# Windowed attention: 256 rows per transfer, manual order, values one block late, and stores moved to another queue

## The chip, the cores and the metric

The kernel runs on one core of a Trainium2 chip; the other cores are idle. Its engines go by the profile's names: PE does the matrix products, ACT and DVE the element-wise work, POOL and SP issue transfers, and 16 DMA engines move the data. A transfer is cut into packets that are spread over these 16; here nearly every data packet is one row of a tile, or two neighbouring rows in e4 and e6. A queue is named by the engine that issues to it. The metric is the device time of one execution in microseconds (us), median of several runs. All runs quoted here of one kernel agree within 0.3%.

## The reference

Attention inside windows of 64 rows, over float32 inputs of shape 4 x 4096 x 1536:

```python
q_w, k_w, v_w = (x.reshape(B, S // 64, 64, D) for x in (q, k, v))      # B, S, D = 4, 4096, 1536
logits = np.einsum('bnwd,bnud->bnwu', q_w, k_w) * D ** -0.5
attn = softmax(logits, axis=-1)
out = np.einsum('bnwu,bnud->bnwd', attn, v_w)
```

Three inputs are read and one output is written, each 100.66 MB: 402.65 MB at the HBM (off-chip memory) in all.

## The kernel before

It handles 128 blocks of 128 rows (two windows). Each block is loaded by three transfers that the POOL engine issues and that convert float32 to float16 on the way. q and k are transposed on PE, their score product is taken for both windows at once, exp is taken of the two 64 x 64 diagonal squares, and the value product is done per window. The store goes out some blocks later, on the POOL queue too.

```python
def load(blk):
    ...                                             # q16, k16, v16: FP16 tiles, 3 buffers
    nc.gpsimd.dma_start(out=q16, in_=qb[blk]...)    # casts float32 -> float16
    nc.gpsimd.dma_start(out=k16, in_=kb[blk]...)
    nc.gpsimd.dma_start(out=v16, in_=vb[blk])

for blk in range(NBLK):                             # NBLK = 128
    ...                                             # load(blk), NPRE = 2 ahead at the start
    if len(pending_store) > 2:
        bs, ts = pending_store.pop(0)
        nc.gpsimd.dma_start(out=ob[bs], in_=ts)     # float32, plain copy
    ...                                             # transposes, scores, exp
    for j in range(D // 512):
        o = o_ps.tile([128, 512], FP32, tag="o", name="o")
        nc.tensor.matmul(o[0:64, :], lhsT=et[0:64, 0:64], rhs=v16[0:64, sl], tile_position=(0, 0), ...)
        nc.tensor.matmul(o[64:128, :], lhsT=et[64:128, 64:128], rhs=v16[64:128, sl], tile_position=(64, 64), ...)
        ...                                         # scaled by 1/sum into out_sb, ACT and DVE in turn
    pending_store.append((blk, out_sb))
for bs, ts in pending_store:                        # the last three
    nc.sync.dma_start(out=ob[bs], in_=ts)
```

The softmax here doesn't subtract the row's maximum and nothing guards it: scores larger than these inputs give would overflow.

## Time and profile before

| | before |
|---|---|
| time, median of 3 runs (the comparison below has a fourth) | 967.0 us |
| span of the profiled run | 964.4 us |
| PE / ACT / DVE busy | 76% / 39% / 31% |
| longest chain | 94% DMA |

From the page of the kernel before: the DMA row over 40 slices of the span (9 is 90% or more busy), the packet counts, the queues (q0 is POOL's, q1 SP's; packets, MB written, share of 16 engines), the HBM traffic and the chain that ended last.

```profile
DMA  9999999999999999999999999999999999999997
DMA packets 73795, 252.60 MB, mean 262 GB/s; under 512 B 8192, under 2 KB 8192, under 8 KB 73728
q0 software_dynamic: 73296, 249.33, 104.6%
q1 hardware_dynamic: 432, 2.36, 0.6%
HBM read 301.99 MB, written 100.66 MB: 417 GB/s over the span
DMA 94%; issue 4%; PE 1%; POOL 0%; DVE 0%; ACT 0%; POOLq 0%; ACTq 0%; DVEq 0%
```

The 16 DMA engines are busy until the last of the 40 slices, so what counts is what they deliver. The 8,192 packets under 512 bytes are completions (16 for each of 512 transfers). The timeline of POOL in the middle of the run (start, duration, engine and line, idle before and what ended it) gives the pace:

```profile
450.27 0.53 POOL L55 DMA_DIRECT2D q<-in_q_dram  x1 [1.22 <-PE o L139]
452.10 0.53 POOL L56 DMA_DIRECT2D k<-in_k_dram  x1 [1.30 <-DMA k<-in_k_dram]
453.96 0.53 POOL L57 DMA_DIRECT2D v<-in_v_dram  x1 [1.33 <-DMA v<-in_v_dram]
455.94 0.54 POOL L86 DMA_DIRECT2D out_dram<-out_sb  x1 [1.45 <-DMA out_dram<-out_sb]
457.86 0.53 POOL L55 DMA_DIRECT2D q<-in_q_dram  x1 [1.38 <-DMA q<-in_q_dram]
```

Four transfers, 786,432 bytes each at the HBM side, take about 7.4 us on average. The end of the run, as busy time by stretch (the last three numbers are PE's granted clock, the DMA share and GB/s written):

```profile
954.00:956.00 2.00, 1.90 (x19) 1.74 (x18) 0.69 (x1) 0.54 (x1) 0.00 (x0) 0.50 0.62 246
956.00:958.00 2.00, 1.56 (x17) 1.22 (x15) 0.69 (x1) 0.71 (x2) 0.00 (x0) 0.79 0.45 183
958.00:960.00 2.00, 1.20 (x8) 0.41 (x8) 0.92 (x2) 1.38 (x4) 0.00 (x0) 1.00 0.05 15
960.00:962.00 2.00, 0.00 (x0) 0.00 (x0) 0.00 (x0) 0.27 (x1) 0.00 (x0) 0.56 0.48 197
```

Here the loads are over, the last block is computed, and the DMA engines run dry until its store.

### The profile page before, as it was taken

What the parts mean: (1) busy time and instruction counts of PE and PEld (TensorE: products, weight loads), DVE (VectorE), ACT (ScalarE), POOL (GpSimd) and SP (SyncE); (2) the same over time, 40 slices, a digit from 0 to 9 for tenths busy, and PEclk for the clock granted to TensorE, in tenths of its full rate; (3) what the DMA queues carried; (4) which work ended last, traced back from release to release, by engine and by line L of the source; (5) the groups of instructions that cost most, each with busy time, mean ns of one, the idle gap of its engine ahead of it and who ended that gap; (6) DMA issues with size and microseconds to landing.
All of it is one profiled execution on the core that took longest, in us unless ns stands there. A gap on an engine that the chain in (4) does not pass through costs nothing.

```text
span 964.4 us, 14246 instructions
## 1 busy us (share of the span) xinstructions
PE 731.4 (76%) x5632; PEld 510.0 (53%) x5632; DVE 294.6 (31%) x515; ACT 378.1 (39%) x641; POOL 271.1 (28%) x514
## 2 busy tenths in 40 slices
PE   5667778787687877877878777777787777878775
PEld 3445555555455555555555555544555555555553
DVE  2323332333333333323233333323332323323332
ACT  3434343433333443434343433344343333344333
POOL 4222222222222222222222322322222222222220
PEclk9776575756756666566575755766656556565655
DMA  9999999999999999999999999999999999999997
GB/s 182 253 270 269 261 261 268 270 262 261 266 270 264 261 266 268 266 262 265 266 267 262 266 264 267 264 266 264 265 267 266 264 264 267 266 264 263 267 268 224
DMA packets 73795, 252.60 MB, mean 262 GB/s; under 512 B 8192, under 2 KB 8192, under 8 KB 73728
## 3 DMA queue, kind: packets, MB, share of 16 engines
q0 software_dynamic: 73296, 249.33, 104.6%
q1 hardware_dynamic: 432, 2.36, 0.6%
q8 instruction: 44, 0.72, 0.3%
q14 instruction: 23, 0.19, 0.0%
HBM read 301.99 MB, written 100.66 MB: 417 GB/s over the span
## 4 chain that ended last, share of the span: by engine, by line
DMA 94%; issue 4%; PE 1%; POOL 0%; DVE 0%; ACT 0%; POOLq 0%; ACTq 0%; DVEq 0%
DMA k<-in_k_dram 92%; DMA q<-in_q_dram 1%; PE tp L95 1%; DVE xt L97 0%; POOL q L55 0%; PE o L135 0%; PE lt L103 0%; PE o L139 0%; POOLq L56 0%; POOL v L57 0%; DVE out_sb L146 0%; ACT out_sb L144 0%; ACT et L112 0%; ACTq L177 0%; PE sp L120 0%
## 5 line engine op out<-in xcount | busy, mean ns | idle before, releaser
L95 PE MATMUL tp<-ident,k 128*128 128x128 f16 x1536 | 327.7, 305 | 139.6 <-DMA k<-in_k_dram 139.6
L95 PE MATMUL tp<-ident,q 128*128 128x128 f16 x1536 | 341.1, 296 | 28.8 <-DMA q<-in_q_dram 12.1
L95 PEld LDWEIGHTS <-k 128*128 128x128 f16 x1536 | 205.9, 139 | 205.3 <-DMA k<-in_k_dram 167.9
L97 DVE COPY xt<-tp 128x1024 f16<-128x1024 f16 x256 | 177.0, 691 | 392.4 <-PE tp L95 392.2
L95 PEld LDWEIGHTS <-q 128*128 128x128 f16 x1536 | 199.8, 137 | 89.8 <-DMA q<-in_q_dram 50.9
L99 ACT COPY xt<-tp 128x1024 f16<-128x1024 f16 x128 | 129.5, 1012 | 287.2 <-PE tp L95 287.2
L144 ACT ACTIVATE out_sb<-o,rs 128x512 f32<-128x512 f32 x256 | 168.6, 685 | 98.7 <-PE o L139 95.1
L103 PE MATMUL lt<-xt 128*128 128x128 f16 x1536 | 192.9, 295 | 3.0 <-DVE xt L97 1.8
L103 PEld LDWEIGHTS <-xt 128*128 128x128 f16 x1536 | 150.6, 136 | 27.4 <-DVE xt L97 26.5
L135 PE MATMUL o<-v,et 64*64 64x512 f16 x384 | 150.6, 502 | 0.0
L139 PE MATMUL o<-v,et 64*64 64x512 f16 x384 | 144.6, 498 | 0.0
L57 POOL DMA_DIRECT2D v<-in_v_dram x128 | 67.9, 530 | 178.1 <-DMA v<-in_v_dram 135.0
L86 POOL DMA_DIRECT2D out_dram<-out_sb x125 | 67.2, 537 | 173.5 <-DMA out_dram<-out_sb 134.0
L112 ACT ACTIVATE et<-lt,zeros 64x64 f16<-64x64 f32 x128 | 39.6, 309 | 192.4 <-PE lt L103 192.4
L56 POOL DMA_DIRECT2D k<-in_k_dram x128 | 67.9, 530 | 162.6 <-DMA k<-in_k_dram 162.6
L55 POOL DMA_DIRECT2D q<-in_q_dram x128 | 68.0, 531 | 156.2 <-PE o L139 124.0
L146 DVE TENSOR_SCALAR out_sb<-o,rs 128x512 f32<-128x512 f32 x128 | 96.0, 750 | 46.6 <-PE o L139 45.1
L129 DVE RECIPROCAL rs<-sp 128x1 f32<-128x1 f32 x128 | 21.5, 168 | 225.5 <-PE sp L124 221.0
L120 PE MATMUL sp<-ones,et 64*64 64x1 f16 x128 | 25.3, 198 | 56.5 <-ACT et L112 56.5
L120 PEld LDWEIGHTS <-et 64*64 64x64 f16 x128 | 14.4, 113 | 86.7 <-ACT et L112 86.2
L139 PEld LDWEIGHTS <-et 64*64 64x64 f16 x384 | 39.4, 132 | 16.8 <-issue 9.8
L135 PEld LDWEIGHTS <-et 64*64 64x64 f16 x384 | 43.5, 126 | 0.4
(12 smaller groups left out, 81.5 us busy)
## 6 DMA issues: line engine op xcount, KB each, us to landing
out_dram<-out_sb POOLq DMA_DIRECT2D x125, 768.0 KB, 14.2
q<-in_q_dram POOLq DMA_DIRECT2D x128, 384.0 KB, 14.3
k<-in_k_dram POOLq DMA_DIRECT2D x128, 384.0 KB, 14.3
v<-in_v_dram POOLq DMA_DIRECT2D x128, 384.0 KB, 14.3
out_dram<-out_sb SPq DMA_DIRECT2D x3, 768.0 KB, 7.8
```

The costliest lines, as they stand in the source:

```text
L55: nc.gpsimd.dma_start(out=q16, in_=qb[blk].rearrange("p (c e) -> p c e", e=128))
L56: nc.gpsimd.dma_start(out=k16, in_=kb[blk].rearrange("p (c e) -> p c e", e=128))
L57: nc.gpsimd.dma_start(out=v16, in_=vb[blk])
L86: nc.gpsimd.dma_start(out=ob[bs], in_=ts)
L95: nc.tensor.transpose(tp[:, i, :], src, ident)
L97: nc.vector.tensor_copy(out=xt[:, g * 8 : g * 8 + 8, :], in_=tp)
L99: nc.scalar.copy(out=xt[:, g * 8 : g * 8 + 8, :], in_=tp)
L103: nc.tensor.matmul(lt[:, 0:128], lhsT=xt[:, 2 * c + 1, :], rhs=xt[:, 2 * c, :], start=(c == 0), stop=(c == DC - 1),)
L135: nc.tensor.matmul(o[0:64, :], lhsT=et[0:64, 0:64], rhs=v16[0:64, sl], tile_position=(0, 0), start=True, stop=True,)
L139: nc.tensor.matmul(o[64:128, :], lhsT=et[64:128, 64:128], rhs=v16[64:128, sl], tile_position=(64, 64), start=True, stop=True,)
L144: nc.scalar.activation(out_sb[:, sl], o, copy_f, bias=0.0, scale=rs)
L146: nc.vector.tensor_scalar_mul(out_sb[:, sl], o, scalar1=rs)
```

## The change

The intent: fewer and larger transfers, more prefetch, PE never waiting for exp, full-size value products, and an end in which stores fill the time that the last blocks need. The core of the diff (shortened: `...` marks what is cut, the `Unit` and `plan` helpers and the reshaped transposes among it; some lines are joined, and the comments after `#` are added here):

```diff
+BODY_G, BODY_R = 2, 1        # 256 rows per transfer; plan() ends with two units of 128 rows
+PREFETCH = 3
...
-    inp = ctx.enter_context(tc.tile_pool(name="inp", bufs=3))
+    inp = ctx.enter_context(tc.tile_pool(name="inp", bufs=PREFETCH + 1))
...
+    ctx.enter_context(tc.manual_schedule())
+    def load(u):
+        for name, src in (("q", qf), ("k", kf), ("v", vf)):
+            t = inp.tile([P, LR, D], FP16, tag=name + "16", name=name + "16")
+            ...
+            nc.gpsimd.dma_start(out=dst, in_=dram(src, u))
...
-            nc.tensor.matmul(o[0:64, :], lhsT=et[0:64, 0:64], rhs=v16[0:64, sl], ...)
-            nc.tensor.matmul(o[64:128, :], lhsT=et[64:128, 64:128], rhs=v16[64:128, sl], ...)
+                    nc.tensor.matmul(o, lhsT=et[:, r, t, :], rhs=u.v[:, g * R + r, sl], ...)  # et zero off the windows
...
-            nc.gpsimd.dma_start(out=ob[bs], in_=ts)
+    def store(i):
+        ...
+        eng = nc.gpsimd if i >= N - PREFETCH - 2 else nc.sync
+        eng.dma_start(out=dram(of, u), in_=src)
+    ...
+    for i, u in enumerate(units):
+        if i + PREFETCH < N:
+            load(units[i + PREFETCH])
+        for g in range(u.G):
+            et = finish_scores(scores(u, g))
+            if prev is not None:
+                pi, pg, pet = prev
+                values(units[pi], pg, pet, False)
+                if pg == units[pi].G - 1:
+                    store(pi)
+            prev = (i, g, et)
+    ...
+    values(units[pi], pg, pet, True)             # the last unit: one store per 512 columns, on SP
```

So the stores of 60 of the 65 units now go to the SP queue; those of the next four go to POOL behind the last loads, and the very last one, in three pieces, to SP.

More of the change, by code (lines that the diff above doesn't have):

```diff
@@ L10, with __init__, plan @@
 FP32 = mybir.dt.float32
+P = 128
+W = 64
+EXP = mybir.ActivationFunctionType.Exp
+COPY = mybir.ActivationFunctionType.Copy
+class Unit:
+    def __init__(self, row0, G, R):
+        self.row0, self.G, self.R = row0, G, R
+        self.rows = P * G * R
+def plan(total):
+    tail = [(1, 1), (1, 1)]
+    units, row = [], 0
+    body = total - sum(P * g * r for g, r in tail)
+    while row < body:
+        units.append(Unit(row, BODY_G, BODY_R))
+        row += units[-1].rows
+    for g, r in tail:
+        units.append(Unit(row, g, r))
+        row += units[-1].rows
+    assert row == total
+    return units
+BODY_G, BODY_R = 2, 1
+PREFETCH = 3
 @with_exitstack
@@ L22 @@
     nc = tc.nc
-    B, S, D, W = q.shape[0], q.shape[1], q.shape[2], 64
-    P = 128
-    DC = D // 128
-    NBLK = (B * S) // P
+    B, S, D = q.shape
+    DC = D // P
+    NJ = D // 512
     scale = float(D) ** -0.5
-    NPRE = 2
-    qb = q.rearrange("b (n p) d -> (b n) p d", p=P)
-    kb = k.rearrange("b (n p) d -> (b n) p d", p=P)
-    vb = v.rearrange("b (n p) d -> (b n) p d", p=P)
-    ob = out.rearrange("b (n p) d -> (b n) p d", p=P)
+    LR = BODY_G * BODY_R
+    qf, kf, vf, of = (x.rearrange("b s d -> (b s) d") for x in (q, k, v, out))
+    units = plan(B * S)
+    N = len(units)
     consts = ctx.enter_context(tc.tile_pool(name="consts", bufs=1))
-    inp = ctx.enter_context(tc.tile_pool(name="inp", bufs=3))
+    inp = ctx.enter_context(tc.tile_pool(name="inp", bufs=PREFETCH + 1))
     xtp = ctx.enter_context(tc.tile_pool(name="xtp", bufs=2))
-    etp = ctx.enter_context(tc.tile_pool(name="etp", bufs=2))
-    outp = ctx.enter_context(tc.tile_pool(name="outp", bufs=6))
-    rsp = ctx.enter_context(tc.tile_pool(name="rsp", bufs=2))
+    outp = ctx.enter_context(tc.tile_pool(name="outp", bufs=4))
+    rsp = ctx.enter_context(tc.tile_pool(name="rsp", bufs=4))
     tp_ps = ctx.enter_context(tc.tile_pool(name="tp_ps", bufs=2, space=bass.MemoryType.PSUM))
@@ L46, with dram @@
     s_ps = ctx.enter_context(tc.tile_pool(name="s_ps", bufs=1, space=bass.MemoryType.PSUM))
-    exp_f = mybir.ActivationFunctionType.Exp
-    copy_f = mybir.ActivationFunctionType.Copy
-    def load(blk):
-        q16 = inp.tile([128, DC, 128], FP16, tag="q16", name="q16")
-        k16 = inp.tile([128, DC, 128], FP16, tag="k16", name="k16")
-        v16 = inp.tile([128, D], FP16, tag="v16", name="v16")
-        nc.gpsimd.dma_start(out=q16, in_=qb[blk].rearrange("p (c e) -> p c e", e=128))
-        nc.gpsimd.dma_start(out=k16, in_=kb[blk].rearrange("p (c e) -> p c e", e=128))
-        nc.gpsimd.dma_start(out=v16, in_=vb[blk])
-        return q16, k16, v16
-    pre = [load(blk) for blk in range(NPRE)]
-    pending_store = []
-    ident = consts.tile([128, 128], FP16, name="ident")
-    ones = consts.tile([128, 8], FP16, name="ones")
-    zeros = consts.tile([128, 1], FP32, name="zeros")
+    def dram(x, u):
+        rows = x[u.row0 : u.row0 + u.rows]
+        return rows.rearrange("(g p r) d -> p g (r d)", g=u.G, p=P, r=u.R)
+    ctx.enter_context(tc.manual_schedule())
+    def load(u):
+        for name, src in (("q", qf), ("k", kf), ("v", vf)):
+            t = inp.tile([P, LR, D], FP16, tag=name + "16", name=name + "16")
+            dst = t[:, : u.G * u.R, :].rearrange("p (g r) d -> p g (r d)", g=u.G)
+            nc.gpsimd.dma_start(out=dst, in_=dram(src, u))
+            setattr(u, name, t)
+    load(units[0])
+    ident = consts.tile([P, P], FP16, name="ident")
+    ones = consts.tile([P, 8], FP16, name="ones")
+    zeros = consts.tile([P, 1], FP32, name="zeros")
     nc.vector.memset(ident, 0.0)
@@ L74 @@
         base=0,
-        pattern=[[-1, 128]],
+        pattern=[[-1, P]],
         channel_multiplier=1,
     )
-    for blk in range(NBLK):
-        if blk < NPRE:
-            q16, k16, v16 = pre[blk]
-        else:
-            q16, k16, v16 = load(blk)
-        if len(pending_store) > 2:
-            bs, ts = pending_store.pop(0)
-            nc.gpsimd.dma_start(out=ob[bs], in_=ts)
-        xt = xtp.tile([128, 2 * DC, 128], FP16, tag="xt", name="xt")
-        for g in range(3):
-            tp = tp_ps.tile([128, 8, 128], FP16, tag="tp", name="tp")
-            for i in range(8):
-                j = g * 8 + i
-                c = j // 2
-                src = q16[:, c, :] if (j % 2 == 0) else k16[:, c, :]
-                nc.tensor.transpose(tp[:, i, :], src, ident)
-            if g != 1:
-                nc.vector.tensor_copy(out=xt[:, g * 8 : g * 8 + 8, :], in_=tp)
-            else:
-                nc.scalar.copy(out=xt[:, g * 8 : g * 8 + 8, :], in_=tp)
-        lt = lt_ps.tile([128, 512], FP32, tag="lt", name="lt")
-        for c in range(DC):
-            nc.tensor.matmul(
-                lt[:, 0:128],
-                lhsT=xt[:, 2 * c + 1, :],
-                rhs=xt[:, 2 * c, :],
-                start=(c == 0),
-                stop=(c == DC - 1),
-            )
-        et = etp.tile([128, 128], FP16, tag="et", name="et")
-        nc.scalar.activation(
-            et[0:64, 0:64], lt[0:64, 0:64], exp_f, bias=zeros[0:64], scale=scale
-        )
-        nc.scalar.activation(
-            et[64:128, 64:128], lt[64:128, 64:128], exp_f, bias=zeros[64:128], scale=scale
-        )
-        sp = s_ps.tile([128, 8], FP32, tag="sp", name="sp")
-        nc.tensor.matmul(
-            sp[0:64, 0:1], lhsT=et[0:64, 0:64], rhs=ones[0:64, 0:1],
-            tile_position=(0, 0), start=True, stop=True,
-        )
-        nc.tensor.matmul(
-            sp[64:128, 0:1], lhsT=et[64:128, 64:128], rhs=ones[64:128, 0:1],
-            tile_position=(64, 64), start=True, stop=True,
-        )
-        rs = rsp.tile([128, 1], FP32, tag="rs", name="rs")
-        nc.vector.reciprocal(out=rs, in_=sp[:, 0:1])
-        out_sb = outp.tile([128, D], FP32, tag="out_sb", name="out_sb")
-        for j in range(D // 512):
-            o = o_ps.tile([128, 512], FP32, tag="o", name="o")
-            sl = slice(512 * j, 512 * (j + 1))
-            nc.tensor.matmul(
-                o[0:64, :], lhsT=et[0:64, 0:64], rhs=v16[0:64, sl],
-                tile_position=(0, 0), start=True, stop=True,
-            )
-            nc.tensor.matmul(
-                o[64:128, :], lhsT=et[64:128, 64:128], rhs=v16[64:128, sl],
-                tile_position=(64, 64), start=True, stop=True,
-            )
-            if j % 2 == 0:
-                nc.scalar.activation(out_sb[:, sl], o, copy_f, bias=0.0, scale=rs)
-            else:
-                nc.vector.tensor_scalar_mul(out_sb[:, sl], o, scalar1=rs)
-        pending_store.append((blk, out_sb))
@@ L150, with scores, mm @@
-    for bs, ts in pending_store:
-        nc.sync.dma_start(out=ob[bs], in_=ts)
+    for u in units[1:PREFETCH]:
+        load(u)
+    ets = {}
+    for R in sorted({u.R for u in units}):
+        ets[R] = []
+        for i in range(2):
+            et = consts.tile([P, R, R, P], FP16, name=f"et{R}{i}")
+            nc.vector.memset(et, 0.0)
+            ets[R].append(et)
+    turn = {R: 0 for R in ets}
+    flip = [0]
+    def scores(u, g):
+        R = u.R
+        per = 8 // (2 * R)
+        xt = xtp.tile([P, DC, 2, LR, P], FP16, tag="xt", name="xt")
+        lt = lt_ps.tile([P, 512], FP32, tag="lt", name="lt")
+        lv = lt[:, : R * R * P].rearrange("p (r s e) -> p r s e", r=R, s=R)
+        def mm(c):
+            for r in range(R):
+                nc.tensor.matmul(
+                    lv[:, r, :, :],
+                    lhsT=xt[:, c, 1, r, :],
+                    rhs=xt[:, c, 0, :R, :],
+                    start=(c == 0),
+                    stop=(c == DC - 1),
+                )
+        done = []
+        for c0 in range(0, DC, per):
+            tp = tp_ps.tile([P, per, 2, R, P], FP16, tag="tp", name="tp")
+            for c in range(c0, c0 + per):
+                for x, src in enumerate((u.q, u.k)):
+                    for r in range(R):
+                        nc.tensor.transpose(
+                            tp[:, c - c0, x, r, :], src[:, g * R + r, c * P : (c + 1) * P], ident
+                        )
+            dst = xt[:, c0 : c0 + per, :, :R, :]
+            if flip[0] % 2 == 0:
+                nc.vector.tensor_copy(out=dst, in_=tp)
+            else:
+                nc.scalar.copy(out=dst, in_=tp)
+            flip[0] += 1
+            done.append(range(c0, c0 + per))
+            if R == 1 and len(done) > 1:
+                for c in done.pop(0):
+                    mm(c)
+        return u, g, xt, lt, lv, mm, done
@@ new lines, in finish_scores @@
+    def finish_scores(state):
+        u, g, xt, lt, lv, mm, done = state
+        R = u.R
+        if R == 1:
+            for cs in done:
+                for c in cs:
+                    mm(c)
+        else:
+            for r in range(R):
+                for c in range(DC):
+                    nc.tensor.matmul(
+                        lv[:, r, :, :],
+                        lhsT=xt[:, c, 1, r, :],
+                        rhs=xt[:, c, 0, :R, :],
+                        start=(c == 0),
+                        stop=(c == DC - 1),
+                    )
+        et = ets[R][turn[R] % 2]
+        turn[R] += 1
+        n = W // R
+        for w in range(P // n):
+            s = slice(w * n, (w + 1) * n)
+            nc.scalar.activation(et[s, :, :, s], lv[s, :, :, s], EXP, bias=zeros[s], scale=scale)
+        return et
@@ new lines, in values @@
+    def values(u, g, et, last):
+        R = u.R
+        if not hasattr(u, "o"):
+            u.o = outp.tile([P, LR, D], FP32, tag="out_sb", name="out_sb")
+        sp = s_ps.tile([P, R, 2], FP32, tag="sp", name="sp")
+        for t in range(R):
+            for r in range(R):
+                nc.tensor.matmul(
+                    sp[:, t, 0:1], lhsT=et[:, r, t, :], rhs=ones[:, 0:1],
+                    start=(r == 0), stop=(r == R - 1),
+                )
+        rs = rsp.tile([P, R], FP32, tag="rs", name="rs")
+        nc.vector.reciprocal(out=rs, in_=sp[:, :, 0])
+        for t in range(R):
+            for j in range(NJ):
+                o = o_ps.tile([P, 512], FP32, tag="o", name="o")
+                sl = slice(512 * j, 512 * (j + 1))
+                for r in range(R):
+                    nc.tensor.matmul(
+                        o, lhsT=et[:, r, t, :], rhs=u.v[:, g * R + r, sl],
+                        start=(r == 0), stop=(r == R - 1),
+                    )
+                dst = u.o[:, g * R + t, sl]
+                if j % 2 == 0:
+                    nc.scalar.activation(dst, o, COPY, bias=0.0, scale=rs[:, t : t + 1])
+                else:
+                    nc.vector.tensor_scalar_mul(dst, o, scalar1=rs[:, t : t + 1])
+                if last:
+                    nc.sync.dma_start(
+                        out=of[u.row0 : u.row0 + u.rows, sl], in_=u.o[:, 0, sl]
+                    )
@@ new lines, in store @@
+    def store(i):
+        u = units[i]
+        src = u.o[:, : u.G * u.R, :].rearrange("p (g r) d -> p g (r d)", g=u.G)
+        eng = nc.gpsimd if i >= N - PREFETCH - 2 else nc.sync
+        eng.dma_start(out=dram(of, u), in_=src)
+    prev = None
+    for i, u in enumerate(units):
[9 more added lines that the diff above has]
+            prev = (i, g, et)
@@ L155 @@
+    pi, pg, pet = prev
+    values(units[pi], pg, pet, True)
 _INS = ['q', 'k', 'v']
```

## The prediction

> **What bounds it now.** The DMA engines. The chain that ended last is 94% DMA (92% on the k loads); no compute engine is busy over 76% (PE; ACT 39%, DVE 31%). The DMA row of the slices stands at 9 until the last slice. Each 128-row block moves three loads and one store of 786 KB on the HBM side; POOL issues one transfer every 1.86 us (POOL timeline, 450 to 475 us), 7.42 us per block, 424 GB/s. So in the span of 964.4 us: 402.65 MB at 423 GB/s (packet records) is 952 us of streaming, 2.8 us precede the first packet, about 1.4 us go at start-up (a dip near 23 us, POOL having waited 5.2 and 2.6 us to issue v loads), about 1 us scattered, and some 6 us at the end: the last load lands near 953.7 us, the DMA share falls to 0.50, 0.10, 0.00, 0.00 between 955 and 961 us, and the last store runs 961 to 963 us.
>
> **What the change does.**
> 1. Half as many body transfers, twice the size. Data packets stay 6,144 bytes at the HBM side; only completion packets are saved. These took 19 ns (mean), one per engine per transfer, beside eight data packets at a pitch of about 229 ns, which makes the 1.86 us; and 229 ns is 192 beats plus three cycles, as the Trainium skill ("DMA: Bandwidth & Descriptors", section Why small descriptors are slow) has it for a packet. Halved: 40 ns of 7,420 per block, 0.54%, 5 us. An estimate, if these packets are serial.
> 2. Stores move to the SP queue: same engines, same bytes. The same page (section Issuing engines are not separate DMA queues) says this saves only issue time. In the tail, where SP stores ran beside POOL loads, packets came at 424 to 430 GB/s: neither gain nor loss.
> 3. Manual order, values one block behind, three 128x128 value products for six 64x64, copies alternating between DVE and ACT. PE per block falls somewhat; ACT rises to about 1.5 x 1.01 + 2 x 0.31 + 2 x 0.66 = 3.5 us. All under 7.4 us per block: off the critical path.
> 4. Prefetch of three 256-row units: the start-up dip (1 us) goes. Small last units, last stores behind the last loads: loads finish earlier, the last compute overlaps some 13 us of stores, and the 6 us tail should become about 3.
>
> **Sum.** 967.0 - 5 - 0 - 1 - 3 - 2 (fewer drops in the stream) = about 956 us. Range 949 to 963. Faster by over 2% would need about 430 GB/s of stream.
>
> **What would show it.** Step 1: the stream at 425 to 426 GB/s, 8,192 completion packets falling to near 4,200, three loads issued per 14.76 us. Step 2: total rate unchanged while a store is in flight. Step 3: PE busy near 650 us, ACT near 440 us, chain still on DMA. Step 4: full DMA share from the first load on, no idle microsecond between last load and last store.
>
> **What would make it wrong.** Two queues alternating on an engine could cost or save per packet (1% is 9.5 us). Reads and writes mixed packet by packet may run slower than in runs of 128. Completion packets may be hidden, so that step 1 gives nothing. If the last units' compute (some 5.5 us per block) lags behind loads that then come every 5.6 us, the tail gains nothing. A slower engine among the 16 would set the pace whatever the queue.

## The result, and the profile after

| | before | after |
|---|---|---|
| time, median | 966.83 us (4 runs) | 969.09 us (4 runs) |
| stream rate, from the packet records | 422.65 GB/s | 419.94 GB/s |
| 402.65 MB at that rate | 952.7 us | 958.8 us |
| lost at the start | 2.0 us | 1.3 us |
| lost at the end | 5.9 us | 2.7 us |

The ratio is 1.0024 (95% interval 1.001 to 1.0038): the same, a hair slower. Every ratio here is the mean time of one kernel's runs over that of the other's of the same rounds, so not quite the ratio of the medians quoted. The prediction of 956 us (949 to 963) was missed.

How the last four rows are made, here and below: every data packet in the records has a start, a duration and a size. Its bytes are counted at the HBM side (6,144 for a load written as 3,072 bytes of float16). The stream rate is the bytes that ended between 100 and 930 us of the records, over that time. A loss is time since the first packet less the bytes so far at the stream rate, at 100 us for the start, and at the last packet less at 930 us for the end. What these rows leave of the time, 6.2 and 6.3 us here and 5.1 to 8.5 us over all runs, lies before the first packet and after the last.

The same lines of the page of the kernel after, with the busy times of the compute engines:

```profile
PE 497.1 (51%) x5120; PEld 369.4 (38%) x5120; DVE 250.5 (26%) x453; ACT 429.9 (44%) x705; POOL 141.5 (15%) x204
DMA  9999999999999999999999999999999999999998
DMA packets 70043, 252.49 MB, mean 261 GB/s; under 512 B 4192, under 2 KB 4192, under 8 KB 69984
q0 software_dynamic: 53232, 156.51, 80.5%
q1 hardware_dynamic: 16752, 95.16, 24.8%
HBM read 301.99 MB, written 100.66 MB: 416 GB/s over the span
```

The completions did fall from 8,192 to 4,192 and the end did fill up, but the HBM rate over the span fell by 1 GB/s. The chain view is of no use after the change: it breaks off at the last ACT instruction. The end of the run, in stretches:

```profile
954.00:956.00 2.00, 1.11 (x9) 0.46 (x8) 0.35 (x2) 1.42 (x3) 0.00 (x0) 1.00 1.01 407
956.00:958.00 2.00, 1.13 (x4) 0.30 (x4) 1.18 (x3) 1.98 (x5) 0.35 (x1) 1.00 0.89 372
958.00:960.00 2.00, 0.00 (x0) 0.00 (x0) 0.21 (x1) 0.51 (x1) 0.21 (x1) 1.00 0.87 363
960.00:962.00 2.00, 0.00 (x0) 0.00 (x0) 0.00 (x0) 0.00 (x0) 0.00 (x0) 0.73 0.99 396
```

Stores keep the engines at 0.87 to 1.01 where before they stood at 0.05 to 0.62. So the start and the end gained 0.7 + 3.2 us, as predicted, and the stream lost 6.1 us instead of gaining 5. In the records, the loss has a place. I cut 70 to 900 us into microseconds, spread each packet's bytes evenly over its duration, and sorted the microseconds by the share of bytes on SP's queue:

| SP's share | microseconds | rate |
|---|---|---|
| none | 344 | 424.8 GB/s |
| 45 to 55% | 350 | 414.7 GB/s |

While no store is in flight, the kernel runs faster than before (424.8 against 422.65); beside a store on SP it runs 2.4% slower. (Single microseconds scatter by 5 to 7 GB/s, so such means are good to some 0.4.) The median time from issue to landing (page, issues by line: size, us) shows how long each store is in flight, out of the 15.0 us of a unit (6.29 MB at 419.94 GB/s):

```profile
out_dram<-out_sb SPq DMA_DIRECT2D x60, 1536.0 KB, 11.8
```

### The profile page after: what moved, and what is told of

It reads as the page before. It is cut to its first block, busy times and chain, and to the rows that moved or that the text cites. A ratio compares the mean times of both kernels' runs of the same rounds, so it can differ in the third digit from the quotient of the medians.

```text
span 967.2 us, 12600 instructions
## 1 busy us (share of the span) xinstructions
PE 497.1 (51%) x5120; PEld 369.4 (38%) x5120; DVE 250.5 (26%) x453; ACT 429.9 (44%) x705; POOL 141.5 (15%) x204
## 2 busy tenths in 40 slices
DMA packets 70043, 252.49 MB, mean 261 GB/s; under 512 B 4192, under 2 KB 4192, under 8 KB 69984
## 5 line engine op out<-in xcount | busy, mean ns | idle before, releaser
L140 PE MATMUL tp<-ident,k 128*128 128x128 f16 x1536 | 252.7, 252 | 244.0 <-DMA k<-in_k_dram 244.0
L147 ACT COPY xt<-tp 128x1024 f16<-128x1024 f16 x192 | 194.3, 1012 | 376.3 <-PE tp L140 376.3
L140 PE MATMUL tp<-ident,q 128*128 128x128 f16 x1536 | 257.5, 251 | 44.3 <-DMA q<-in_q_dram 44.3
L140 PEld LDWEIGHTS <-k 128*128 128x128 f16 x1536 | 176.2, 116 | 270.6 <-DMA k<-in_k_dram 261.5
L145 DVE COPY xt<-tp 128x1024 f16<-128x1024 f16 x192 | 132.8, 691 | 439.8 <-PE tp L140 438.0
L126 PEld LDWEIGHTS <-xt 128*128 128x128 f16 x1536 | 109.6, 110 | 224.3 <-ACT xt L147 159.0
L177 ACT ACTIVATE et<-lt,zeros 64x64 f16<-64x64 f32 x256 | 79.2, 309 | 148.4 <-PE sp L187 143.6
L198 PE MATMUL o<-v,et 128*128 128x512 f16 x384 | 116.9, 417 | 0.5 <-ACT out_sb L204 0.5
L198 PEld LDWEIGHTS <-et 128*128 128x128 f16 x384 | 30.9, 104 | 19.6 <-issue 7.0
L187 PEld LDWEIGHTS <-et 128*128 128x128 f16 x128 | 14.1, 110 | 0.6 <-ACT et L177 0.6
L216 POOL DMA_DIRECT2D out_dram<-out_sb x4 | 2.7, 679 | 22.1 <-ACT out_sb L204 18.8
```

What stands on the lines that cost most here:

```text
L126: nc.tensor.matmul(lv[:, r, :, :], lhsT=xt[:, c, 1, r, :], rhs=xt[:, c, 0, :R, :], start=(c == 0), stop=(c == DC - 1),)
L140: nc.tensor.transpose(tp[:, c - c0, x, r, :], src[:, g * R + r, c * P : (c + 1) * P], ident)
L145: nc.vector.tensor_copy(out=dst, in_=tp)
L147: nc.scalar.copy(out=dst, in_=tp)
L177: nc.scalar.activation(et[s, :, :, s], lv[s, :, :, s], EXP, bias=zeros[s], scale=scale)
L187: nc.tensor.matmul(sp[:, t, 0:1], lhsT=et[:, r, t, :], rhs=ones[:, 0:1], start=(r == 0), stop=(r == R - 1),)
```

## The experiments

Theory A says that two queues side by side cost: each DMA engine takes packets from POOL's and SP's queues in turn, and the turn costs time. Rivals: B, the manual order or the late values cost it; C, 256-row transfers are slower in themselves. The times of all runs, with the stream rates from the packet records:

| run | what it is | time, us | stream, GB/s | ratio to before |
|---|---|---|---|---|
| after | | 969.09 | 419.94 | 1.0024 |
| e1 | after, stores on POOL | 959.37 | 424.55 | 0.9928 |
| e2 | before, stores on SP | 977.14 | 418.53 | 1.011 |
| e3 | e1, v on SP, cast by ACT | 1055.74 | not steady | 1.0919 |
| e4 | e1, two rows per partition | 953.64 | 427.94 | 0.9868 |
| e5 | e1, 128-row transfers | 966.79 | 422.81 | 1.0001 |
| e6 | e4, stores on SP | 958.67 | 426.13 | 0.9918 |
| e7 | e1, v on SP, no cast needed | 965.66 | 421.96 | 0.9991 |
| e8 | after, last stores on SP too | 971.69 | 419.93 | 1.005 |
| e9 | e1, all loads uncast, prefetch of two | 970.71 | 419.34 | 1.0043 |
| e10 | e9, stores on SP | 969.09 | 420.29 | 1.0027 |
| e11 | e9, v on SP | 970.01 | 420.30 | 1.0036 |
| e12 | e1, values at once | 958.73 | 424.62 | 0.992 |
| e13 | e9, loads converted to float32r | 971.57 | 420.03 | 1.0051 |
| e14 | e13, stores on SP | 973.86 | 418.14 | 1.0077 |

The kernel before took 966.4 to 966.5 us beside each of e1 to e14, and 966.83 beside the change.

### e1: all stores back on POOL

```diff
-        eng = nc.gpsimd if i >= N - PREFETCH - 2 else nc.sync
+        eng = nc.gpsimd
```

> The changed kernel with one edit: every store but the last unit's goes to the POOL queue, as before the change; the data transfers, the order of the compute instructions and the tail stay. Theory A (two queues): in the changed kernel the packet rate was 425 GB/s in microseconds without a store and 415 GB/s where 30 to 60% of the bytes were stores, so the loss comes from each engine alternating between the POOL and the SP queue. Then the stream should run at 425 GB/s throughout, and the time be about 969 - 402.65 MB x (1/420 - 1/425.5) = 969 - 12 = 957 us (954 to 960). Rival B (order): the manual order or the values one block behind cost the time; then it stays at 969, as those are untouched. Rival C (size): 256-row transfers are slower in themselves, then it stays near 969 too.

959.37 us, 9.7 us less than the change, with all its other parts in place; B and C fall as causes of the loss. The page shows all transfers but the last unit's stores on one queue, and a higher HBM rate:

```profile
q0 software_dynamic: 69552, 250.89, 105.2%
q1 hardware_dynamic: 432, 0.79, 0.2%
HBM read 301.99 MB, written 100.66 MB: 421 GB/s over the span
```

POOL's timeline is even, one transfer of twice the size every 3.7 us:

```profile
499.56 0.71 POOL L84 DMA_DIRECT2D q<-in_q_dram  x1 [2.90 <-DMA q<-in_q_dram]
503.23 0.71 POOL L84 DMA_DIRECT2D k<-in_k_dram  x1 [2.96 <-DMA k<-in_k_dram]
506.88 0.72 POOL L84 DMA_DIRECT2D v<-in_v_dram  x1 [2.94 <-DMA v<-in_v_dram]
510.70 0.72 POOL L216 DMA_DIRECT2D out_dram<-out_sb  x1 [3.10 <-ACT xt L147]
514.33 0.71 POOL L84 DMA_DIRECT2D q<-in_q_dram  x1 [2.90 <-DMA q<-in_q_dram]
```

### e2: the kernel before with its stores on SP

```diff
-            nc.gpsimd.dma_start(out=ob[bs], in_=ts)
+            nc.sync.dma_start(out=ob[bs], in_=ts)
```

> The kernel before with one edit: its 125 stores in the loop go to the SP queue. Theory A: slower by what two queues cost, with stores in flight about half of the time at 2% less: 967 + 9 = about 976 us (972 to 982). Rivals B and C: nothing they speak of is touched, so 967 us.

977.14 us, 10.7 us more than before. The same move costs about the same in a kernel with none of the change's other parts: 9.4 us of it is stream, and the end loses 7.9 us instead of 5.9. Without SP packets it ran at 421.0 GB/s, with 45 to 55% of them at 416.5.

```profile
q0 software_dynamic: 55296, 151.02, 78.9%
q1 hardware_dynamic: 18432, 100.67, 26.1%
HBM read 301.99 MB, written 100.66 MB: 413 GB/s over the span
```

### e3: v loads on SP, cast later (a failed design)

```diff
-            nc.gpsimd.dma_start(out=dst, in_=dram(src, u))
+            eng = nc.sync if name == "v" else nc.gpsimd     # v: float32 tile; and e1's edit
+            eng.dma_start(out=dst, in_=dram(src, u))
...
+        v16 = xtp.tile([P, R, D], FP16, tag="v16c", name="v16c")
+        nc.scalar.copy(out=v16, in_=u.v[:, g * R : (g + 1) * R, :])
```

> All stores on the POOL queue as in e1, but the v loads go to the SP queue, uncast (float32 in SBUF, cast by ACT later, 1.5 us more of ACT per block, still under 5.5 of 7.4 us). Now two queues run side by side and both read from HBM. Theory A1 (any alternation of queues on an engine costs): stream near 415 to 420 GB/s, about 970 us. Theory A2 (only alternation of a load with a store, packet by packet, costs): mostly load beside load, so near 424 GB/s, about 958 us.

1055.74 us, but not by the queues. I had put the cast on ACT right in front of the value product. The view of waits (who waited for what: us in total, times, longest) shows PE waiting for the cast, and POOL, which issues q and k behind each store, waiting for the results:

```profile
POOL out_dram L219 <- ACT out_sb L207: 776.9, 63, 15.2
PE o L201 <- ACT v16c L184: 292.5, 128, 2.6
```

The queues ran dry and the run settles nothing about them; e7 repairs it.

### e4: two neighbouring rows per partition, stores on POOL

```diff
-BODY_G, BODY_R = 2, 1
+BODY_G, BODY_R = 1, 2          # and e1's edit
```

> All stores on POOL, and two neighbouring rows per partition (the code's R = 2 path), so that each descriptor covers 12,288 bytes at the HBM side instead of 6,144. If the 3 cycles or so of overhead per packet[...] are per descriptor, the stream gains 0.75% more than e1, about 950 us; if the hardware cuts the descriptor into the same packets, it equals e1. PE does more (256-column score products, twice the value products), some 6 of 14.8 us more per 256 rows, which should stay hidden.

The 3 cycles are those of step 1 of the prediction.

953.64 us, the fastest version here, 1.3% under before. The stream gained 0.80% on e1, 7.5 us, where 0.75% was expected; the time gained only 5.7, as the end lost 4.6 us instead of 2.8. The same bytes went in about half as many packets:

```profile
DMA packets 37786, 252.51 MB, mean 265 GB/s; under 512 B 4192, under 2 KB 4192, under 8 KB 29664
HBM read 301.99 MB, written 100.66 MB: 423 GB/s over the span
```

PE's busy time rose to 660 us and stayed hidden. Three streams now give the costs on one DMA engine. A 128-row transfer is 8 data packets and a completion: 786,432 bytes / 422.65 GB/s = 1.861 us. A 256-row one is 16 and one: 1,572,864 / 424.55 = 3.705 us. The difference over 8 is 230.5 ns a packet, which leaves 17 ns for the completion and whatever else comes once per transfer (the completion's mean recorded duration is 19). With two rows per packet: (1,572,864 / 427.94 - 17 ns) / 8 = 457.3 ns, or 3.7 ns less than two packets. The Trainium skill ("DMA: Bandwidth & Descriptors", section Why small descriptors are slow) gives a fixed overhead of about 3 cycles per packet; at the 850 MHz that this page states for the fabric, an estimate of 3.5 ns. The three streams fix just these three unknowns, so the sums do not check themselves; the 19 ns and the page's figure are the only outside checks.

### e5: e1 with 128-row transfers

```diff
-BODY_G, BODY_R = 2, 1
+BODY_G, BODY_R = 1, 1          # and e1's edit
```

> e1 with 128-row transfers in the body (BODY_G = 1), prefetch of three such. From the streams of the kernel before (422.6 GB/s, 8 packets per engine and transfer) and e1 (424.5, 16 packets), one packet takes 230.5 ns and the completion 17 ns. Theory: size is worth only the completion packet, so this streams at 422.6 GB/s and takes 402.65 MB x (1/422.6 - 1/424.5) = 4.3 us more than e1, 963 to 964 us. Rival: the gain of e1 over before came from the tail and start alone and size gives nothing; then it equals e1, 959.4.

966.79 us, 3 us more than expected. The stream, 422.81 GB/s, is as expected: 952.3 us against e1's 948.4. Most of the rest is the end, which lost 5.0 us instead of 2.8, probably because three units of 128 rows ahead leave fewer stores to fill it. So size itself is worth some 4 us, and no part of it hurts.

### e6: e4 with the stores on SP

```diff
-BODY_G, BODY_R = 2, 1
+BODY_G, BODY_R = 1, 2          # stores as in the changed kernel
```

> e4 (two rows per partition, 12,288-byte packets) with the stores on SP as in the changed kernel. The two queues cost the changed kernel 10.2 us of stream against e1 (420.0 against 424.5 GB/s). If alternation costs a fixed time per packet, half as many packets cost half: 953.6 + 5 = 958.7. If it costs a share of the rate (reads beside writes), the full 10: 963.9.

958.67 us, 5.0 us over e4, where the change is 9.7 over e1. Half as many packets cost half: the toll goes with the packets and is not a share of the rate, which would have cost the full 10. That the total hit the expected 958.7 is partly luck: only 4.0 of the 5.0 us is stream (940.9 to 944.9 us, against 10.4 us for the change over e1), the rest lies at the ends and outside the packets. In time, an engine's packet pitch is 16 engines x bytes / rate: in the changed kernel 16 x 6,144 / 424.8 = 231.4 ns without SP and 237.1 at 414.7, so 5.7 ns a packet. In e6 it is 459.5 ns (427.9 GB/s) and 463.8 (423.9), so 4.3 ns. By the error of such means (0.4 GB/s) the two differ, so the toll per packet is similar, but not shown to be constant.

### e7: v loads on SP, without the cast

```diff
+            eng = nc.sync if name == "v" else nc.gpsimd     # v: float32 tile
+            eng.dma_start(out=dst, in_=dram(src, u))
...                                                    # e1's edit; bfloat16 for ones and et
+            if name == "v":                                # upper 16 bits, read as bfloat16
+                t = t.bitcast(BF16).rearrange("p l (d two) -> p l d two", two=2)[:, :, :, 1]
```

> e3 repaired: stores on POOL, v loads as float32 on SP, and no cast: the value product reads the upper 16 bits of v as bfloat16 (so slightly less exact, on purpose), so that no engine has more to do than in e1. Theory A1 (any alternation of two queues on an engine costs): where SP carries about half of the packets, beside other loads, the rate falls to about 415 GB/s as in the changed kernel, and the time is near 968. Theory A2 (only a load alternating with a store costs): 424 GB/s there, about 960. Either way the microseconds without SP packets should show 424 to 425.

965.66 us: 6.3 over e1, nearer A1 than A2. But split by what ran beside SP's v loads, it surprised. In microseconds where SP had 45 to 55%:

| beside SP's float32 loads | microseconds | rate |
|---|---|---|
| POOL's casting loads (stores under 30%) | 234 | 418.0 GB/s |
| POOL's stores for 30 to 70% of the bytes | 117 | 422.7 GB/s |

A load beside a store cost little, a load beside a casting load cost much, so A2 falls. Neither had I foreseen that A1 holds beside one kind of packet only. (That split was made after the run, so e10, e11 and e14 had to test what it suggests.) The new theory, A4: the toll is for packets that convert in alternation with packets that do not.

### e8: the changed kernel with its last stores on SP too

```diff
-        eng = nc.gpsimd if i >= N - PREFETCH - 2 else nc.sync
+        eng = nc.sync
```

> The changed kernel with the last stores on SP too, so no longer behind the last loads. Theory: the tail's gain (5.8 us lost to the stream's rate at the end before, 2.7 us after) came from that order; then about 3 us longer than the changed kernel, 971 to 973. Rival: it came from the small last units and the split last store, which stay; then 969.

971.69 us, 2.6 over the change; the stream is the same, and the end loses 6.0 us instead of 2.7. The hole is back:

```profile
958.00:960.00 2.00, 1.69 (x16) 1.33 (x14) 0.69 (x1) 0.73 (x1) 0.00 (x0) 0.50 0.54 196
960.00:962.00 2.00, 1.32 (x15) 0.94 (x13) 0.09 (x1) 1.08 (x2) 0.00 (x0) 0.82 0.40 159
962.00:964.00 2.00, 1.34 (x7) 0.32 (x5) 0.93 (x4) 1.95 (x5) 0.00 (x0) 1.00 0.00 0
```

The order of stores and loads made the gain at the end; the small last units, which stay here, do not make it alone. (e8's runs spread from 970.11 to 972.78 us, so the 2.6 is rough; the loss at the end is of its profiled run, 972.18.)

### e9, e10, e11: no load converts

All loads are left as float32 and read as bfloat16 (less exact). e9 has everything on POOL, e10 the stores on SP as in the change, e11 the v loads on SP (e9 and e11 with e1's edit). For all three:

```diff
-PREFETCH = 3
+PREFETCH = 2                                    # for room
-            t = inp.tile([P, LR, D], FP16, tag=name + "16", name=name + "16")
+            t = inp.tile([P, LR, D], FP32, tag=name + "32", name=name + "32")
...
+            t = t.bitcast(BF16).rearrange("p l (d two) -> p l d two", two=2)[:, :, :, 1]
```

> Control for the next two: q, k and v all loaded uncast (float32 in SBUF, read as bfloat16 through their upper 16 bits, less exact on purpose), all loads and stores on POOL, prefetch of two units instead of three for room. HBM bytes and packet sizes at the HBM side as in e1, so about 424.5 GB/s and 959 us, if the write side of a load (6,144 instead of 3,072 bytes) is not what a packet waits for.

970.71 us: wrong by 12. An uncast load on one queue is slower, 419.34 GB/s, though it reads the same bytes from HBM. I had no reason for this, and have none. The shorter prefetch is not it: loads here took 28 to 29 us from issue to landing (median), nearly two units of 15 us, so the queue did not run dry.

> As the control, with the stores on SP as in the changed kernel. In e7 float32 loads on SP beside stores on POOL ran at 422.7 GB/s, beside casting loads at 418. Theory A1 (any alternation of two queues costs per packet): 415 to 418 GB/s in the microseconds with stores, 8 to 10 us more than the control. Theory A4 (only the alternation of packets that cast with packets that do not costs): 423 or more there, within 3 us of the control.

969.09 us, 1.6 less than its control. In microseconds with 45 to 55% on SP it ran at 423.4 GB/s, without SP at 417.0. The toll is not only gone, it has turned into a gain. Its two queues:

```profile
q0 software_dynamic: 52960, 305.93, 76.4%
q1 hardware_dynamic: 17024, 96.74, 23.9%
```

> As the control, with the v loads on SP: two queues, both with uncast loads, now and then a POOL store. A1: 417 to 418 GB/s where SP has half of the packets, as in e7 (418), some 6 us more than the control. A4: 422 to 425 there, within 3 us of the control.

970.01 us, 0.7 less than its control; 421.2 GB/s with 45 to 55% on SP, 419.5 without. Two queues as such cost nothing here, so A1 falls.

### e12: values at once

```diff
             et = finish_scores(scores(u, g))
-            if prev is not None:
-                ...                              # values of the block before
+            values(u, g, et, i == N - 1)
...                                              # store(i) follows; and e1's edit
```

> e1 with the value product of a block right after its scores instead of one block later, the rest of the order as it was. If DMA alone sets the pace in the stream, PE's extra waits for exp are hidden: 959 us as e1, give or take 1. If the order mattered, PE would fall behind the 7.4 us of a block and the time rise above 965.

958.73 us, 0.6 less than e1. Putting the values one block behind gains nothing, as no compute engine sets the pace.

### e13, e14: conversion or size

A casting load of float16 also writes half as many bytes as a plain packet, and unequal sizes might be the cause (A5). A load into a float32r tile is a conversion by its types and keeps the size: its packets are recorded with 6,144 bytes. Otherwise e13 is e9 and e14 is e10.

```diff
-            t = inp.tile([P, LR, D], FP32, tag=name + "32", ...)
+            t = inp.tile([P, LR, D], mybir.dt.float32r, tag=name + "32", ...)
```

> e9 with the load tiles declared float32r: the loads then convert (float32 to float32r) but write as many bytes as they read. Control for the next run. If the conversion costs nothing alone, 970.7 us as e9; if it is the conversion that makes loads in one queue run at 424.5 instead of 419.3 GB/s, 959.

971.57 us, near e9: this conversion does not make the single queue faster.

> e10 with float32r load tiles, stores on SP: converting loads of 6,144 written bytes alternate with plain stores of 6,144. If conversion beside plain copies is what costs (theory A4), the rate with stores in flight falls 8 to 10 GB/s below the rate without, and the run takes 8 to 10 us more than its control e13. If it is the unequal written size (3,072 beside 6,144, theory A5), it behaves as e10 did: 969 us, and the rate with stores in flight not below that without.

973.86 us. By the microseconds the answer is plain: 422.5 GB/s without SP packets, 413.5 with 45 to 55% of them, a loss of 9.0 GB/s in the size that A4 named, with all packets at 6,144 bytes. A5 falls. e10 differs in the tiles' type alone and moved the same packets, yet e14 took 4.8 us more, and its packets a larger share of the engines' time:

```profile
q0 software_dynamic: 52960, 305.93, 80.8%
q1 hardware_dynamic: 17024, 96.74, 25.3%
```

The totals against e13 show less, 2.3 us against the expected 8 to 10, as the control, too, ran at only 420.0 GB/s. Loads and stores cannot be told apart in e13's records (same queue, same size), so why the control is no faster stays open.

The three pairs together, with loads on POOL and stores on SP:

| loads | rate without SP packets | with 45 to 55% on SP | toll |
|---|---|---|---|
| float32 to float16 (after) | 424.8 | 414.7 | 10.1 GB/s |
| float32 to float32r (e14) | 422.5 | 413.5 | 9.0 GB/s |
| not converted (e10) | 417.0 | 423.4 | none |

The packet records (100 to 900 us) hold one more witness. The recorded duration of a plain store packet of 6,144 bytes has a median of 234 ns in e1 and e10, but of 247 in the changed kernel and 248 in e14. The longer ones (243 ns and more) make up 94% of them in the changed kernel and in e14, and 1.5% in e10's SP queue. In one queue with casting loads they are 1 in 8 in the kernel before and 1 in 16 in e1, which is one for each engine and transfer. So the longer record seems to mark a plain packet right behind a converting one, in one queue as well; two queues make almost every store packet such a one. Records overlap, so 13 ns is not itself the toll, but on half of the packets it would be 6.5 ns per packet, near the 5.7 from the rates.

## Why the prediction was wrong

- **What bounds it: right.** Every run but e3 is the bytes at the stream rate, the losses at the two ends, and 5.1 to 8.5 us outside all packets. Waiting less on PE (e12's order against e1's) is worth nothing.
- **Step 1, larger transfers: right.** Predicted 5 us; the stream of e1 is 952.7 - 948.4 = 4.3 us shorter than that of before, and e5 ties it to the size. That it is the completion rests on 17 ns by difference beside 19 ns recorded.
- **Step 2, stores on SP, "neither gain nor loss": this is the step that failed.** It cost 958.8 - 948.4 = 10.4 us of stream, a toll of some 6 ns for each packet while casting loads alternate with stores. I had read 424 to 430 GB/s from two microseconds of the tail where SP stores ran beside POOL loads. At 16 engines and 6,144 bytes, one packet more or less in a microsecond is 6 GB/s, so this window could not resolve a loss of 10 (cut from the start of the span, the two microseconds with the first of these stores read 427 and 419); I had also named the risk and then given it no weight in the range. The skill's sentence that issuing from several engines saves issue time was read as "costs nothing".
- **Step 3, off the critical path: right,** but PE's size was off: 497 us busy instead of 650. PE's mean granted clock was 0.794 in the profiled run instead of 0.632, which is probably why: e5, with the same 5,120 matmuls at a clock of 0.662, was busy for 648 us. ACT came to 430 us (predicted 440).
- **Step 4, start and end: right.** Start 0.7 us (predicted 1), end 3.2 us (predicted 3); e8 shows that the gain at the end hangs on the order of the stores.
- **"Fewer drops in the stream", 2 us: wrong.** Before, the 83 stretches of 10 us between 100 and 930 us ran at 419.6 to 424.5 GB/s: no drop stood out that could have been removed. Without steps 2 and this, the sum 967.0 - 4.3 - 0.7 - 3.2 gives 958.8, and e1 measured 959.4.

What stays open: how a DMA engine spends the 6 ns, and why plain loads in one queue are slower than plain loads and stores in two (e9, e10). That in two queues the toll comes with converting packets beside plain ones, and not with plain beside plain, is shown; the mechanism is not. Whether such alternation inside one queue costs as much, no run tried.

## What to carry to other kernels

Where the DMA engines are the bound, look at the packet rate by what is in flight, not only at the share of busy time, which read 9 in all but the last slice in both kernels. If loads convert on the way, as here, keep the stores on the same queue as long as the stream is full, and queue the last stores behind the last loads. To gain more, lengthen the contiguous run that a packet covers (two rows per partition gave 5.7 us over e1), which also halves the number of packets that a toll can fall on (e6).

## What the Trainium skill lacked or had wrong

- "DMA: Bandwidth & Descriptors", section Issuing engines are not separate DMA queues, says that spreading transfers over issuing engines only saves the sequencer's time. Converting POOL loads beside plain SP stores ran at 414.7 GB/s instead of 424.8, and moving the stores cost 9.7 us (after against e1) and 10.7 us (e2 against before). With plain loads the mix was faster, 423.4 against 417.0.
- The same page, section Why small descriptors are slow, treats the overhead as a matter of small descriptors, and packing several of them into one packet as worth it only at 256 bytes or less. Its 3 cycles agree with the 3.7 ns measured; what it lacks is that one row of 12,288 bytes in place of two of 6,144 still gave 427.94 against 424.55 GB/s.
- The same page, section Anatomy of one DMA, puts the semaphore write at about one cycle, next to nothing. In a full queue a transfer took some 17 ns of each engine beside its data, worked out above from the gain of 256-row transfers (424.55 against 422.65 GB/s), and the completion's own record is 19 ns.
- No page that I read says that an uncast float32 load in one queue is slower than a casting one: 419.34 (e9) against 424.55 GB/s (e1).
